# Sending two of every sixteen row tiles from HBM to HBM, one register-addressed row per DMA, in a rank-and-scatter kernel that is bound by its DMA engines

## The chip, the cores and the metric

The kernel runs on one core of one Trainium2 chip. The metric is the device time of one execution, in microseconds, and lower is better. A run of several executions is given by its median. SP, ACT, Pool and VectorE are engines of the core; the sequencers of SP, ACT and Pool, which run their instructions, also issue the DMAs. Sixteen DMA engines move the data in packets. A DMA has landed when the last of its sixteen completion counts, one from each DMA engine, has arrived.

## The reference

```python
def setup_inputs():
    B, N, D = 8, 2048, 2560
    return {"x": np.random.randn(B, N, D).astype(np.float32),
            "scores": np.random.randn(B, N).astype(np.float32)}

def reference(x, scores):
    ranks = np.argsort(np.argsort(scores, axis=1), axis=1)
    out[b_idx, ranks, :] = x        # out has the shape of x
```

Row `i` of a batch goes to row `rank(score i)` of the output. There are 16,384 rows of 2,560 floats (10,240 bytes), so 167.8 MB are read and 167.8 MB written. The arithmetic is small; the kernel is a permutation of rows.

## The kernel before

The scores are spread over all partitions, and VectorE counts for each row of a 128-row tile how many scores precede it. One tile takes three comparisons with an accumulator and three small instructions that join the counts:

```python
    def compute_ranks_for_batch(b):
        for k in range(T):                      # T = 16 tiles of P = 128 rows
            ... tensor_scalar(is_lt, add)  -> accA   # later scores
            ... tensor_scalar(is_le, add)  -> accB   # earlier scores
            ... scalar_tensor_tensor       -> accC   # ties inside the tile
            ... tensor_tensor(add) twice   -> rank_f32[:, col]
            nc.vector.tensor_copy(out=ranks_i32[:, col:col+1], in_=rank_f32[:, col:col+1])
```

The data path is a load into SBUF, issued by SP, and a scatter, issued by Pool, whose row addresses are the ranks:

```python
    for b in range(B):
        for t in range(T):
            xt = x_pool.tile([P, D], fp32, tag="x")          # 13 buffers
            nc.sync.dma_start(out=xt[:], in_=x[b, P*t:P*(t+1), :])
            nc.gpsimd.indirect_dma_start(                    # cut
                out=out_flat, out_offset=IndirectOffsetOnAxis(ap=ranks_i32[:, col:col+1], axis=0),
                in_=xt[:], element_offset=b*N*D, ...)
```

Of the kernel before, what the change touches and what calls it, by code (L numbers as in the profile page):

```python
# [10 lines left out]
@with_exitstack  # L11
def kernel(
    ctx: ExitStack,
    tc: tile.TileContext,
    x: bass.AP,
    scores: bass.AP,
    out: bass.AP,
):
    nc = tc.nc
    fp32 = mybir.dt.float32  # L20
    i32 = mybir.dt.int32

    B, N, D = x.shape
    P = 128
    T = N // P

    out_flat = out.flatten_outer_dims()

    const_pool = ctx.enter_context(tc.tile_pool(name="const", bufs=1))
    rank_pool = ctx.enter_context(tc.tile_pool(name="rank", bufs=1))  # L30
    NXBUF = 13
    x_pool = ctx.enter_context(tc.tile_pool(name="x", bufs=NXBUF))
    psum_pool = ctx.enter_context(tc.tile_pool(name="bc_psum", bufs=8, space=bass.MemoryType.PSUM))

    s_all = const_pool.tile([P, B * N], fp32, name="s_all")
    s_col = const_pool.tile([P, B * T], fp32, name="s_col")
    NR = B * T
    s_rows = const_pool.tile([NR, P], fp32, name="s_rows")
    ones128 = const_pool.tile([P, P], fp32, name="ones128")
    tri128 = const_pool.tile([P, P], fp32, name="tri128")  # L40
    ident128 = const_pool.tile([P, P], fp32, name="ident128")
    trash = const_pool.tile([P, N], fp32, name="trash")

    accA = rank_pool.tile([P, B * T], fp32, name="accA")
    accB = rank_pool.tile([P, B * T], fp32, name="accB")
    accC = rank_pool.tile([P, B * T], fp32, name="accC")
    rank_f32 = rank_pool.tile([P, B * T], fp32, name="rank_f32")
    ranks_i32 = rank_pool.tile([P, B * T], i32, name="ranks_i32")

    nc.sync.dma_start(  # L50
        out=s_rows[:],
        in_=scores.rearrange("b (k p) -> (b k) p", p=P),
    )

    nc.gpsimd.memset(ones128[:], 1.0)  # L55
    nc.gpsimd.affine_select(  # L56
        out=tri128[:],
        in_=ones128[:],
        pattern=[[-1, P]],
        compare_op=mybir.AluOpType.is_ge,  # L60
        fill=0.0,
        base=-1,
        channel_multiplier=1,
    )
    make_identity(nc, ident128[:])

    scol_psum = psum_pool.tile([P, 512], fp32, tag="bc")
    nc.tensor.transpose(  # L68
        out=scol_psum[:, :NR],
        in_=s_rows[:],  # L70
        identity=ident128[:NR, :NR],
    )
    nc.scalar.copy(out=s_col[:], in_=scol_psum[:, :NR])  # L73

    GRP = 4
    n_groups = (T + GRP - 1) // GRP
    for b in range(B):
        for g in range(n_groups):
            k_lo = GRP * g
            k_hi = min(T, k_lo + GRP)  # L80
            nk = k_hi - k_lo
            bc_psum = psum_pool.tile([P, 512], fp32, tag="bc")
            for j in range(nk):
                k = k_lo + j
                col = b * T + k
                nc.tensor.transpose(  # L86
                    out=bc_psum[:, P * j: P * (j + 1)],
                    in_=s_col[:, col:col + 1].to_broadcast([P, P]),
                    identity=ident128[:],
                )  # L90
            nc.scalar.copy(  # L91
                out=s_all[:, b * N + P * k_lo: b * N + P * k_hi],
                in_=bc_psum[:, :P * nk],
            )

    def compute_ranks_for_batch(b):
        base = b * N
        for k in range(T):
            col = b * T + k
            sc = s_col[:, col:col + 1]  # L100
            nc.vector.tensor_scalar(  # L101
                out=trash[:, :N - P * k],
                in0=s_all[:, base + P * k: base + N],
                scalar1=sc,
                scalar2=None,
                op0=mybir.AluOpType.is_lt,
                op1=mybir.AluOpType.add,
                accum_out=accA[:, col:col + 1],
            )
            if k > 0:  # L110
                nc.vector.tensor_scalar(  # L111
                    out=trash[:, :P * k],
                    in0=s_all[:, base: base + P * k],
                    scalar1=sc,
                    scalar2=None,
                    op0=mybir.AluOpType.is_le,
                    op1=mybir.AluOpType.add,
                    accum_out=accB[:, col:col + 1],
                )
            nc.vector.scalar_tensor_tensor(  # L120
                out=trash[:, :P],
                in0=s_all[:, base + P * k: base + P * (k + 1)],
                scalar=sc,
                in1=tri128[:],
                op0=mybir.AluOpType.is_equal,
                op1=mybir.AluOpType.mult,
                accum_out=accC[:, col:col + 1],
            )
            if k > 0:
                nc.vector.tensor_tensor(  # L130
                    out=rank_f32[:, col:col + 1],
                    in0=accA[:, col:col + 1],
                    in1=accB[:, col:col + 1],
                    op=mybir.AluOpType.add,
                )
                nc.vector.tensor_tensor(  # L136
                    out=rank_f32[:, col:col + 1],
                    in0=rank_f32[:, col:col + 1],
                    in1=accC[:, col:col + 1],
                    op=mybir.AluOpType.add,  # L140
                )
            else:
                nc.vector.tensor_tensor(  # L143
                    out=rank_f32[:, col:col + 1],
                    in0=accA[:, col:col + 1],
                    in1=accC[:, col:col + 1],
                    op=mybir.AluOpType.add,
                )
            nc.vector.tensor_copy(  # L149
                out=ranks_i32[:, col:col + 1],  # L150
                in_=rank_f32[:, col:col + 1],
            )

    for b in range(B):
        compute_ranks_for_batch(b)

    span = B * N * D
    for b in range(B):
        for t in range(T):
            col = b * T + t  # L160
            xt = x_pool.tile([P, D], fp32, name=f"xt_{b}_{t}", tag="x")
            nc.sync.dma_start(out=xt[:], in_=x[b, P * t: P * (t + 1), :])  # L162
            scatter_out = dataclasses.replace(
                out_flat[:], dep_tracking_offset=col * span
            )
            nc.gpsimd.indirect_dma_start(  # L166
                out=scatter_out,
                out_offset=bass.IndirectOffsetOnAxis(
                    ap=ranks_i32[:, col:col + 1], axis=0
                ),  # L170
                in_=xt[:],
                in_offset=None,
                element_offset=b * N * D,
            )


# [28 lines left out]
```

## Time and profile before

| | before |
|---|---|
| median | 796.45 us (796.38 to 796.53, 2 runs) |
| bytes through the DMA engines | 335.75 MB, 429 GB/s in all but the first and last slice |
| VectorE / Pool / ACT / PE busy | 49% / 15% / 2% / 2% |

These are lines of the page of the kernel before: the busy tenths and the GB/s in 40 equal slices of the span, the DMA queues (packets, MB, share of the time of 16 engines), the chain of waits that ended last by line, and the DMA issues (count, KB each, median us from issue to landing).

```profile
DVE  6999999999999999999900000000000000000000
DMA  8999999999999999999999999999999999999996
GB/s 345 429 429 428 429 428 429 429 428 429 428 428 428 429 428 429 428 428 429 428 429 429 429 429 429 429 429 429 429 429 429 428 429 429 429 429 430 429 429 260
q1 hardware_dynamic: 18576, 167.85, 50.0%
q0 software_dynamic: 18432, 167.78, 49.8%
DMA xt<-in_x_dram 96%; SPq L162 0%; POOLq L200 0%; SPq L50 0%; POOLq L166 0%
xt<-in_x_dram SPq DMA_DIRECT2D x128, 1280.0 KB, 48.8
out_dram<-xt,ranks_i POOLq DMA_INDIRECT x128, 28.2
```

The DMA engines work without a gap. SP's loads and Pool's scatters take half of them each, because every byte passes twice. A DMA lands 28 to 49 us after its issue and nobody minds: the buffers keep enough of them in flight.

### The profile page before, as it was taken

The page shows a single profiled execution, that of the slowest core. Times are in us where ns is not written, and L with a number is a line of the kernel's source. Part 1 is how long each engine was busy: PE and PEld are TensorE (multiplying, and loading weights), DVE is VectorE, ACT ScalarE, POOL GpSimd, SP SyncE. Part 2 cuts the span into 40 slices and gives each one's busy share as a digit, 9 for nine tenths or more (in the row PEclk, how much of TensorE's full clock was granted, in tenths as well). Part 3 has the DMA queues.
Part 4 walks back from the last instruction along what each step waited for, and adds up shares of the span by engine and source line. Part 5 has one row for each costly group of instructions (what it writes and reads, how often), then busy time and mean ns, then how long its engine had stood idle before and what let it go on. Part 6 is the DMA issues. An engine that isn't in the chain of part 4 may idle for free.

```text
span 794.8 us, 1987 instructions
## 1 busy us (share of the span) xinstructions
PE 15.9 (2%) x129; PEld 15.4 (2%) x129; DVE 388.0 (49%) x1128; ACT 17.5 (2%) x34; POOL 123.0 (15%) x136
## 2 busy tenths in 40 slices
PE   7000000000000000000000000000000000000000
PEld 7000000000000000000000000000000000000000
DVE  6999999999999999999900000000000000000000
ACT  8000000000000000000000000000000000000000
POOL 1211111111111111111111111111111111111110
PEclk9555555555555555555555555555555555555555
DMA  8999999999999999999999999999999999999996
GB/s 345 429 429 428 429 428 429 429 428 429 428 428 428 429 428 429 428 428 429 428 429 429 429 429 429 429 429 429 429 429 429 428 429 429 429 429 430 429 429 260
DMA packets 37023, 335.75 MB, mean 422 GB/s; under 512 B 4113, under 2 KB 4241, under 8 KB 4241
## 3 DMA queue, kind: packets, MB, share of 16 engines
q1 hardware_dynamic: 18576, 167.85, 50.0%
q0 software_dynamic: 18432, 167.78, 49.8%
q14 instruction: 14, 0.11, 0.0%
q8 instruction: 1, 0.02, 0.0%
HBM read 167.84 MB, written 167.77 MB: 422 GB/s over the span
## 4 chain that ended last, share of the span: by engine, by line
DMA 96%; another core or an unknown queue 1%; SPq 1%; issue 0%; POOLq 0%
DMA xt<-in_x_dram 96%; SPq L162 0%; POOLq L200 0%; SPq L50 0%; POOLq L166 0%
## 5 line engine op out<-in xcount | busy, mean ns | idle before, releaser
L166 POOL DMA_INDIRECT out_dram<-xt,ranks_i x128 | 121.9, 952 | 656.7 <-DMA xt<-in_x_dram 425.4
L101 DVE TENSOR_SCALAR_CACHE_REDUCE trash<-s_all,s_col 128x2048 f32<-128x2048 f32 (+15 forms) x128 | 172.1, 1345 | 8.0 <-ACT s_all L91 7.6
L111 DVE TENSOR_SCALAR_CACHE_REDUCE trash<-s_all,s_col 128x128 f32<-128x128 f32 (+14 forms) x120 | 153.5, 1279 | 0.0
L120 DVE SCALAR_TENSOR_TENSOR trash<-s_all,s_col,tri 128x128 f32<-128x128 f32 x128 | 45.0, 351 | 0.4
L149 DVE CAST ranks_i<-rank_f 128x1 int32<-128x1 f32 x128 | 19.0, 149 | 0.0
L130 DVE TENSOR_TENSOR rank_f<-accA,accB 128x1 f32<-128x1 f32 x120 | 18.7, 156 | 0.0
L136 DVE TENSOR_TENSOR rank_f<-rank_f,accC 128x1 f32<-128x1 f32 x120 | 18.6, 155 | 0.0
L91 ACT COPY s_all<-bc_psum 128x512 f32<-128x512 f32 x32 | 16.0, 749 | 1.7 <-PE bc_psum L86 1.7
L86 PE MATMUL bc_psum<-ident,s_col 128*128 128x128 f32 x128 | 15.4, 286 | 0.4 <-ACT s_col L73 0.4
L86 PEld LDWEIGHTS bc_psum<-ident,s_col 128*128 128x128 f32 x128 | 15.2, 146 | 0.6 <-ACT s_col L73 0.6
L120 DVE DVE_READ_ACCUMULATOR trash<-s_all,s_col,tri 128x1 f32 x128 | 10.6, 83 | 0.0
L101 DVE DVE_READ_ACCUMULATOR trash<-s_all,s_col 128x1 f32 x128 | 10.5, 82 | 0.0
L111 DVE DVE_READ_ACCUMULATOR trash<-s_all,s_col 128x1 f32 x120 | 9.9, 83 | 0.0
L73 ACT ACT_TABLE_LOAD x1 | 1.3, 1283 | 0.8 <-PEq L189 0.8
L143 DVE TENSOR_TENSOR rank_f<-accA,accC 128x1 f32<-128x1 f32 x8 | 1.3, 159 | 0.0
L68 PE MATMUL scol_psum<-ident,s_rows 128*128 128x128 f32 x1 | 0.4, 448 | 2.9 <-DMA s_rows<-in_scores_dram 2.9
L73 ACT COPY s_col<-scol_psum 128x128 f32<-128x128 f32 x1 | 0.3, 266 | 1.3 <-PE scol_psum L68 1.3
L56 POOL TENSOR_SCALAR_AFFINE_SELECT tri<-ones 128x128 f32<-128x128 f32 x1 | 0.3, 283 | 0.0
masks.py:199 POOL TENSOR_SCALAR_AFFINE_SELECT ident<-ident 128x128 f32<-128x128 f32 x1 | 0.3, 282 | 0.0
L55 POOL MEMSET ones<- 128x128 f32 x1 | 0.2, 205 | 0.3 <-POOLq L189 0.3
L68 PEld LDWEIGHTS scol_psum<-ident,s_rows 128*128 128x128 f32 x1 | 0.2, 183 | 2.9 <-issue 2.9
masks.py:197 POOL MEMSET ident<- 128x128 f32 x1 | 0.2, 202 | 0.0
(4 smaller groups left out, 0.4 us busy)
## 6 DMA issues: line engine op xcount, KB each, us to landing
xt<-in_x_dram SPq DMA_DIRECT2D x128, 1280.0 KB, 48.8
out_dram<-xt,ranks_i POOLq DMA_INDIRECT x128, 28.2
s_rows<-in_scores_dram SPq DMA_DIRECT2D x1, 64.0 KB, 2.0
```

Of the source, the lines that this page charges most:

```text
L68: nc.tensor.transpose(out=scol_psum[:, :NR], in_=s_rows[:], identity=ident128[:NR, :NR],)
L73: nc.scalar.copy(out=s_col[:], in_=scol_psum[:, :NR])
L86: nc.tensor.transpose(out=bc_psum[:, P * j: P * (j + 1)], in_=s_col[:, col:col + 1].to_broadcast([P, P]), identity=ident128[:],)
L91: nc.scalar.copy(out=s_all[:, b * N + P * k_lo: b * N + P * k_hi], in_=bc_psum[:, :P * nk],)
L101: nc.vector.tensor_scalar(out=trash[:, :N - P * k], in0=s_all[:, base + P * k: base + N], scalar1=sc, scalar2=None, op0=mybir.AluOpType.is_lt,
L111: nc.vector.tensor_scalar(out=trash[:, :P * k], in0=s_all[:, base: base + P * k], scalar1=sc, scalar2=None, op0=mybir.AluOpType.is_le, op1 ...
L120: nc.vector.scalar_tensor_tensor(out=trash[:, :P], in0=s_all[:, base + P * k: base + P * (k + 1)], scalar=sc, in1=tri128[:], op0=mybir.Alu ...
L130: nc.vector.tensor_tensor(out=rank_f32[:, col:col + 1], in0=accA[:, col:col + 1], in1=accB[:, col:col + 1], op=mybir.AluOpType.add,)
L136: nc.vector.tensor_tensor(out=rank_f32[:, col:col + 1], in0=rank_f32[:, col:col + 1], in1=accC[:, col:col + 1], op=mybir.AluOpType.add,)
L143: nc.vector.tensor_tensor(out=rank_f32[:, col:col + 1], in0=accA[:, col:col + 1], in1=accC[:, col:col + 1], op=mybir.AluOpType.add,)
L149: nc.vector.tensor_copy(out=ranks_i32[:, col:col + 1], in_=rank_f32[:, col:col + 1],)
L166: nc.gpsimd.indirect_dma_start(out=scatter_out, out_offset=bass.IndirectOffsetOnAxis(ap=ranks_i32[:, col:col + 1], axis=0), in_=xt[:], in_ ...
```

## The change

The intent is to take bytes off the bottleneck. Two of the sixteen tiles of each batch (2,048 rows in all) no longer go through SBUF: each row is one DMA from `x` in HBM to its place in `out` in HBM, so its bytes pass the engines once. The target row sits in a register, loaded sixteen at a time. SP issues the rows of one tile and ACT those of the other. Pool issues loads and scatters of the other 112 tiles ("the bulk").

```diff
-    NXBUF = 13
+    NXBUF = 12
     ...
+    DIRECT = (T - 2, T - 1)
+    G = 16
     for b in range(B):
-        compute_ranks_for_batch(b)
+        compute_ranks(b, DIRECT)
+        ... transpose the two rank columns to rows_i[2, P], cast to int32
+        compute_ranks(b, BULK)
+
+    def direct_rows(eng, et, b, q, g):
+        _, vals = nc.values_load_multi_w_load_instructions(
+            rows[b][q:q + 1, G * g: G * (g + 1)], engines=[et], ...)
+        for i in range(G):
+            r = P * DIRECT[q] + G * g + i
+            o = dataclasses.replace(out[b, bass.ds(vals[i], 1), :], ...)
+            eng.dma_start(out=o, in_=x[b, r:r + 1, :])
     ... (cut: load(k) and scatter(k) now both on nc.gpsimd)
+    with tc.manual_schedule(engines={ACT, SPE, POOLE}):
+        for k in range(LEAD): load(k)                 # LEAD = 8
+        for k in range(len(bulk)):
+            if k + LEAD < len(bulk): load(k + LEAD)
+            scatter(k)
+        for b in range(B):
+            for g in range(P // G):
+                direct_rows(nc.sync, SPE, b, 0, g)
+                direct_rows(nc.scalar, ACT, b, 1, g)
```

More of the change, by code (lines that the diff above doesn't have):

```diff
@@ L94, with compute_ranks @@
             )
-    def compute_ranks_for_batch(b):
+    def compute_ranks(b, tiles):
         base = b * N
-        for k in range(T):
+        for k in tiles:
             col = b * T + k
@@ L152, in compute_ranks_for_batch @@
             )
-    for b in range(B):
-        compute_ranks_for_batch(b)
-    span = B * N * D
-    for b in range(B):
-        for t in range(T):
-            col = b * T + t
-            xt = x_pool.tile([P, D], fp32, name=f"xt_{b}_{t}", tag="x")
-            nc.sync.dma_start(out=xt[:], in_=x[b, P * t: P * (t + 1), :])
-            scatter_out = dataclasses.replace(
-                out_flat[:], dep_tracking_offset=col * span
-            )
-            nc.gpsimd.indirect_dma_start(
-                out=scatter_out,
-                out_offset=bass.IndirectOffsetOnAxis(
-                    ap=ranks_i32[:, col:col + 1], axis=0
-                ),
-                in_=xt[:],
-                in_offset=None,
-                element_offset=b * N * D,
-            )
+    span = B * N * D
@@ new lines @@
+    ACT = mybir.EngineType.Activation
+    SPE = mybir.EngineType.SP
+    DIRECT = (T - 2, T - 1)
+    BULK = [t for t in range(T) if t not in DIRECT]
+    G = 16
+    drow_pool = ctx.enter_context(tc.tile_pool(name="drow", bufs=2))
+    rows = []
+    for b in range(B):
+        compute_ranks(b, DIRECT)
+        rp = psum_pool.tile([P, 512], fp32, tag="bc", name=f"rp_{b}")
+        rows_i = drow_pool.tile([len(DIRECT), P], i32, tag="rows", name=f"rows_{b}")
+        nc.tensor.transpose(
+            out=rp[:len(DIRECT), :P],
+            in_=rank_f32[:, b * T + DIRECT[0]: b * T + T],
+            identity=ident128[:],
+        )
+        nc.vector.tensor_copy(out=rows_i[:], in_=rp[:len(DIRECT), :P])
+        rows.append(rows_i)
+        compute_ranks(b, BULK)
@@ new lines, in direct_rows @@
+    def direct_rows(eng, et, b, q, g):
+        _, vals = nc.values_load_multi_w_load_instructions(
+            rows[b][q:q + 1, G * g: G * (g + 1)],
+            engines=[et],
+            min_val=0,
+            max_val=N - 1,
+            skip_runtime_bounds_check_because=(
+                "a rank counts other scores of one row of N, so it lies in 0..N-1"
+            ),
+        )
+        t = DIRECT[q]
+        for i in range(G):
+            r = P * t + G * g + i
+            o = dataclasses.replace(
+                out[b, bass.ds(vals[i], 1), :],
+                dep_tracking_offset=(B * T + b * N + r) * span,
+            )
+            eng.dma_start(out=o, in_=x[b, r:r + 1, :])
@@ new lines, with load, scatter @@
+    POOLE = mybir.EngineType.Pool
+    bulk = [(b, t) for b in range(B) for t in BULK]
+    LEAD = 8
+    xts = {}
+    def load(k):
+        b, t = bulk[k]
+        xts[k] = x_pool.tile([P, D], fp32, name=f"xt_{b}_{t}", tag="x")
+        nc.gpsimd.dma_start(out=xts[k][:], in_=x[b, P * t: P * (t + 1), :])
+    def scatter(k):
+        b, t = bulk[k]
+        col = b * T + t
+        nc.gpsimd.indirect_dma_start(
+            out=dataclasses.replace(
+                out_flat[:], dep_tracking_offset=col * span
+            ),
+            out_offset=bass.IndirectOffsetOnAxis(
+                ap=ranks_i32[:, col:col + 1], axis=0
+            ),
+            in_=xts.pop(k)[:],
+            in_offset=None,
+            element_offset=b * N * D,
+        )
@@ L178 @@
+    with tc.manual_schedule(engines={ACT, SPE, POOLE}):
+        for k in range(LEAD):
+            load(k)
+        for k in range(len(bulk)):
+            if k + LEAD < len(bulk):
+                load(k + LEAD)
+            scatter(k)
[3 more added lines that the diff above has]
+                direct_rows(nc.scalar, ACT, b, 1, g)
 _INS = ['x', 'scores']
```

## The prediction

Its sums came to 683 + 74 + 14, about 770 us, with the rows hidden, and otherwise to about 755 us for the bulk and a tail of 25 to 180 us. The numbers it starts from are in the trace of the kernel before: bulk packets start 381 ns apart, pieces of 512 bytes take 27 ns and semaphore packets 9, and of 28,234 packets of loads and scatters between 100 and 700 us, 99% were followed on their engine by a packet of the other queue (strung together by their times, as in part 5).

> **What bounds the kernel now.** The chain of waits is 96% DMA of the row-tile loads; the 40-slice table shows the DMA engines at 9 tenths throughout and 429 GB/s, while DVE is busy 49%, POOL 15%, ACT and PE 2%. Each byte passes the DMA engines twice (load, scatter). The packet records show why: each of the 16 engines moves 10,240-byte packets 381 ns apart, 2 x 128 tiles x 8 = 2,048 per engine = 781 us; about 14 us is start and end.
>
> **What the change does.** 112 of 128 tiles keep the double trip: 1,792 packets x 381 ns = 683 us per engine, now all on Pool's queue (8 DMAs in flight, each about 3.05 us of engine time, so that queue should not run dry; Pool's 224 issues of about 0.95 us cost it about 213 us, hidden). 2,048 rows pass once, each as 16 pieces of 640 bytes plus 16 semaphore packets. The 512-byte pieces of the scores load took 27 ns, semaphore packets 9 ns in slots of about 6; I estimate 30 + 6 ns per row and engine, 74 us. Sum 683 + 74 + 14 = about 770 us (-3.3%), if the direct rows are hidden entirely beside the bulk. DVE does the same comparisons (3.05 us per tile, done near 390 us); the eight extra transposes and casts are negligible. DVE's casts of batches 2 and 3 wait for the direct rows of batches 0 and 1 to be read; at my cadence these are done in time.
>
> **The direct rows' own pace decides.** SP and ACT must issue 1,024 rows each in about 735 us: 0.72 us per row. Limits:
> - Turns. In the packet records, the load queue and the scatter queue alternate strictly, packet by packet, and a semaphore packet takes a turn of its own. A direct row then needs two turns, each behind one Pool packet: with 2,016 Pool packets in all (semaphores included), about 0.75 us per row. Bulk ends with at best about 985 of 1,024 rows done on each queue.
> - Window. The built program lets each queue have four rows in flight (each issue waits for the fourth before it). Unloaded pieces: issue 0.33-0.42 us, 0.63 us to the first packet, 0.3-0.5 us from semaphore packet to landing. That fits, but the first scatter needed 3.8 us from issue end to first packet under load. If rows meet that, the cadence exceeds 1 us.
> - Register loads: one of 16 values per 16 rows.[...]
>
> So bulk should end near 755 us and a tail of 40 to 300 direct rows per queue follow at about 0.6 us (issue bound): 25 to 180 us. If data and semaphore share a turn, no tail: 770. A design this finely balanced suggests somebody tuned it to win, so I pull the middle down: 800 us, range 762 to 900; faster 0.38, same 0.24, slower 0.38.
>
> **What would show it.** Right: DMA slices below 9 tenths at the end, with Pool's queue finished and only SP/ACT rows left; DMA-issue median of a direct row about 3 us; SP waiting on its own DMAs. Share of engine time of the direct queues about 9-10%; total bytes 315 MB. Wrong on the good side: SP and ACT finish before Pool, DMA at 9 tenths to the end.
>
> **What would make it wrong.** [...]register-addressed issue well over 0.5 us (slower); 640-byte HBM-to-HBM pieces costing more than 30 ns (slower); packets joined (faster); DVE blocked on the casts, starving scatters (slower).

## The result

| | before | after |
|---|---|---|
| median | 796.45 us | 1,166.88 us (1,165.41 to 1,168.36, 2 runs) |
| bytes | 335.75 MB | 315.31 MB |
| bulk finished at | 792 us | 758 us |
| direct rows issued by then, of 1,024 | | SP 524, ACT 510 |

The ratio is 1.465 (95% interval 1.461 to 1.470). A ratio here is the mean time of one kernel's runs over that of the other's runs of the same rounds, so it is not quite the ratio of the medians quoted. (The end of the bulk is the start of its last packet in the trace.)

The same lines of the page of the changed kernel, which has one queue more; the chain is here given by engine:

```profile
DVE  7999996999995950000000000000000000000000
DMA  9999999999999999999999999511111111111111
GB/s 373 411 422 421 421 422 421 422 421 423 420 421 423 420 422 422 422 419 398 385 372 390 386 382 397 231 27 26 27 27 26 27 27 26 27 27 26 27 27 20
q0 software_dynamic: 32256, 293.62, 61.0%
q1 hardware_dynamic: 32912, 10.62, 4.3%
q10 hardware_dynamic: 32768, 10.55, 4.2%
DMA 56%; ACTq 18%; DVE 4%; issue 3%; PE 0%; ACT 0%; DVEq 0%
out_dram<-in_x_dram SPq DMA_DIRECT2D x1024, 10.0 KB, 4.9
out_dram<-in_x_dram ACTq DMA_DIRECT2D x1024, 10.0 KB, 2.4
```

The reader should see two kernels in this page. Until slice 26 the engines are full, much as before. Then they move 27 GB/s for 400 us: only direct rows are left. The medians 4.9 and 2.4 mix the two stages, and must be taken apart. The next lines are the direct rows' issues in the window 100 to 500 us, with their median time to landing:

```profile
out_dram<-in_x_dram SPq DMA_DIRECT2D x300, 10.0 KB, 5.1
out_dram<-in_x_dram ACTq DMA_DIRECT2D x292, 10.0 KB, 5.2
```

and the same for 540 to 700 us, where the bulk itself ran slower, with the total of that window:

```profile
DMA packets 13070, 61.44 MB, mean 384 GB/s; under 512 B 3995, under 2 KB 7276, under 8 KB 7276
out_dram<-in_x_dram SPq DMA_DIRECT2D x106, 10.0 KB, 5.9
out_dram<-in_x_dram ACTq DMA_DIRECT2D x100, 10.0 KB, 6.2
```

and for 770 to 1,150 us, with no bulk:

```profile
DMA packets 31117, 10.19 MB, mean 27 GB/s; under 512 B 15546, under 2 KB 31095, under 8 KB 31095
out_dram<-in_x_dram SPq DMA_DIRECT2D x486, 10.0 KB, 1.9
out_dram<-in_x_dram ACTq DMA_DIRECT2D x486, 10.0 KB, 2.0
```

300 rows in 400 us is one row per 1.33 us; 486 in 380 us is one per 0.78 us. Beside the bulk a row lands 5.2 us after its issue, and with four rows in flight on a queue (the built program gives each queue four completion semaphores, and an issue waits for the fourth before it; in the trace SP's 1,024 issues use four semaphores, 256 each) the next can be issued every 5.2 / 4 = 1.3 us. That this is what SP waits for is in its own waits (total us, number, longest):

```profile
SPq L193 <- DMA out_dram<-in_x_dram: 277.0, 313, 2.8
```

After the bulk the latency is 2.0 us and the window would allow 0.5 us. Now the sequencer is the limit: 517 ns for an issue (524 on ACT), about 0.7 us with the register arithmetic and gaps, and one register load of 0.97 us (1.02 on ACT) per sixteen rows, which makes 0.78 us. The sum closes: 758 us, plus 510 rows times 0.78 us, is 1,156 us against a span of 1,163.7 us.

The first theory was therefore **W**, the window: latency beside the bulk over four. Rivals were **Q**, SP and ACT hindering each other in something they share; **T**, turns, each direct row waiting for its turns behind bulk packets; and a path of the memory made slow by the scatters' writes.

### The profile page after: what moved, and what is told of

It is laid out like the page before. It is cut to its first block, busy times and chain, and to the rows that moved or that the text cites. A ratio compares the mean times of both kernels' runs of the same rounds, so it can differ in the third digit from the quotient of the medians.

```text
span 1163.7 us, 8140 instructions
## 1 busy us (share of the span) xinstructions
PE 19.7 (2%) x137; PEld 17.1 (1%) x137; DVE 390.0 (34%) x1136; ACT 17.8 (2%) x34; POOL 172.4 (15%) x232
## 2 busy tenths in 40 slices
DMA packets 97999, 315.31 MB, mean 271 GB/s; under 512 B 36368, under 2 KB 69264, under 8 KB 69264
## 4 chain that ended last, share of the span: by engine, by line
DMA 56%; ACTq 18%; DVE 4%; issue 3%; PE 0%; ACT 0%; DVEq 0%
DMA out_dram<-in_x_dram 55%; ACTq L193 15%; ACTq L177 4%; DVE trash L101 2%; DVE trash L111 2%; DVE trash L120 0%; PE bc_psum L86 0%; DMA s_rows<-in_scores_dram 0%; DVE rank_f L130 0%; DVE rank_f L136 0%; DVE ranks_i L149 0%; DVE rows L172 0%; ACT s_all L91 0%; PE scol_psum L68 0%; ACT s_col L73 0%
## 5 line engine op out<-in xcount | busy, mean ns | idle before, releaser
L101 DVE TENSOR_SCALAR_CACHE_REDUCE trash<-s_all,s_col 128x256 f32<-128x256 f32 (+15 forms) x128 | 172.2, 1345 | 8.3 <-ACT s_all L91 7.9
L111 DVE TENSOR_SCALAR_CACHE_REDUCE trash<-s_all,s_col 128x1792 f32<-128x1792 f32 (+14 forms) x120 | 153.4, 1279 | 0.0
L203 POOL DMA_DIRECT2D xt<-in_x_dram x112 | 60.4, 541 | 491.2 <-DMA out_dram<-xt,ranks_i 488.6
L208 POOL DMA_INDIRECT out_dram<-xt,ranks_i x112 | 110.9, 990 | 69.3 <-issue 27.6
L167 PE MATMUL rp<-ident,rank_f 128*2 128x128 f32 x8 | 2.9, 359 | 361.8 <-DVE rank_f L136 361.8
```

What stands on the lines that cost most here:

```text
L101: nc.vector.tensor_scalar(out=trash[:, :N - P * k], in0=s_all[:, base + P * k: base + N], scalar1=sc, scalar2=None, op0=mybir.AluOpType.is_lt,
L111: nc.vector.tensor_scalar(out=trash[:, :P * k], in0=s_all[:, base: base + P * k], scalar1=sc, scalar2=None, op0=mybir.AluOpType.is_le, op1 ...
L203: nc.gpsimd.dma_start(out=xts[k][:], in_=x[b, P * t: P * (t + 1), :])
L208: nc.gpsimd.indirect_dma_start(out=dataclasses.replace(out_flat[:], dep_tracking_offset=col * span), out_offset=bass.IndirectOffsetOnAxis( ...
```

## The experiments

Eighteen kernels ran. "Wrong" marks kernels that leave out work to isolate a cost. A latency is from the start of the issue to the landing, and a cadence is the mean distance of two rows' issues on one queue, both from the trace. Unless noted, edits are against the changed kernel.

### 1. The rows alone, and the bulk alone

`direct_only` (wrong on purpose, one look):

```diff
     with tc.manual_schedule(...):
-        for k in range(LEAD): load(k)
-        for k in range(len(bulk)): ... load(k + LEAD); scatter(k)
         for b in range(B): ... direct_rows(...)
```

> Wrong result on purpose: the bulk is left out, only the 2,048 direct rows are moved. My theory (W): while Pool's 10,240-byte packets fill the DMA engines a row takes about 5.2 us from issue to landing, and with four rows in flight per queue that makes 1.3 us per row; without them the sequencer's own work decides (0.52 us DMA issue + 0.18 us register work and gaps + 1.0 us register load per 16 rows = 0.78 us per row), on SP and ACT at once. So 0.78 us per row from the first row on, latency 1.9 to 2.1 us, span 38 + 1,024 x 0.78 + a few = about 845 us (825 to 870), that is, longer than the whole kernel before. Rival (Q): SP and ACT [...]hold each other up, or the rows are slow in themselves: cadence stays near 1.3 us and the span near 1,370 us.

Measured: 842.31 us. The latency was 2.0 us and the cadence 0.78 us from the start to the end, as in the changed kernel's tail. The direct rows in the window 100 to 500 us:

```profile
out_dram<-in_x_dram SPq DMA_DIRECT2D x503, 10.0 KB, 2.0
out_dram<-in_x_dram ACTq DMA_DIRECT2D x502, 10.0 KB, 2.0
```

Both queues run at full pace beside each other, so Q falls. And this settles something more basic: 1,024 rows per queue need 1,024 x 0.78 = 800 us even on an idle machine. The design could not win at two tiles per batch, whatever the bulk did.

`bulk_only` (wrong on purpose, one look):

```diff
-                direct_rows(nc.sync, SPE, b, 0, g)
-                direct_rows(nc.scalar, ACT, b, 1, g)
+                pass
```

> Wrong result on purpose: the direct rows are left out, 112 tiles go through Pool alone. 1,792 packets x 381 ns = 683 us + 14 us = about 698 us (690 to 705) at 429 GB/s throughout, if the bulk's slower stretch from 520 to 730 us in the changed kernel comes from the direct rows beside it. If it belongs to the bulk (its queue or its addresses), the dip is here too and the span is 715 to 735 us.

Measured: 698.83 us, at 429 GB/s throughout. The bulk's packet sum in the prediction was right (683 + 14 = 697), and Pool issuing both directions costs nothing. There was no slow stretch either, so that of the changed kernel (384 GB/s from 540 to 700 us) comes with the rows or with their instructions.

### 2. Packet size and turns

`half_packets` (correct, one look) cuts the bulk's rows into packets of 5,120 bytes:

```diff
-        nc.gpsimd.dma_start(out=xts[k][:], in_=x[b, ...])
+        nc.gpsimd.dma_start(out=xts[k][:], in_=x[b, ...], max_dma_last_dim=4 * (D // 2))
     ... and two scatters a tile, of half rows, with ranks 2r and 2r + 1
```

> The changed kernel with every bulk row cut in two pieces of 5,120 bytes, for loads and scatters; the direct rows are as they were. Theory W with packets counted: a newly issued row stands behind a fixed number of Pool packets already taken up by the engine (3.3 us from end of issue to first packet = 8 to 9 packets of 381 ns). Halved packets then halve that: first packet about 1.7 us after issue, latency about 3.2 us, cadence 0.8 to 0.9 us while the bulk runs, total 880 to 960 us. Rival (T), turns alone as I predicted: two turns of about 0.2 us per row, so the issue bound of 0.78 us holds at once and the total is about 845 us. Rival (M), a latency of memory or fabric under load that does not depend on packet size: nothing changes, cadence 1.3 us, total about 1,165 us.

Measured: 1,222.06 us, far above the 880 to 960 expected; latency 5.8 to 5.9 us on SP (6.0 on ACT), cadence 1.55 to 1.67 us. The bulk ended at 763 us, 5 us later than in the changed kernel, and only 448 to 456 rows of a queue were issued by then. If a row waited for a fixed number of bulk packets, halving the packets would have halved the wait. It did not, so a fixed number of packets falls, and with it T in its plain form.

`single_packet` (correct, one look) asks for the row's DMA to be one packet, so that its data and its semaphore might share a turn:

```diff
-            eng.dma_start(out=o, in_=x[b, r:r + 1, :])
+            eng.dma_start(out=o, in_=x[b, r:r + 1, :], single_packet=True)
```

> The changed kernel with the option single_packet set on the direct rows, meant to put the 640-byte piece and its semaphore into one packet, so that a row takes one turn per engine and not two. If turns are a large part of the 5.2 us (I estimate 0.8 to 1.6 us of it), the latency beside the bulk falls to 3.6 to 4.4 us and the cadence to 0.9 to 1.1 us, total 960 to 1,060 us. If the start delay (3.2 us from end of issue to the first packet) is what counts and is not shortened, 4.8 to 5.2 us and 1,120 to 1,165 us.

Measured: 1,168.43 us, latency 5.2 us, cadence 1.34 us, and the same 97,999 packets on its page: no change. The option joined no packets, so this run says nothing about turns; `half_packets` is what speaks against them. The prediction's hope for "packets joined" was empty.

### 3. The window itself

`one_tile` (correct, 5 rounds) makes one tile per batch direct, shared by SP and ACT:

```diff
-    DIRECT = (T - 2, T - 1)
+    DIRECT = (T - 1,)
     ...
-            for g in range(P // G):
+            for g in range(0, P // G, 2):
                 direct_rows(nc.sync, SPE, b, 0, g)
-                direct_rows(nc.scalar, ACT, b, 1, g)
+                direct_rows(nc.scalar, ACT, b, 0, g + 1)
```

> One direct tile per batch in place of two, its rows shared by SP and ACT: 512 rows on each queue. Theory W: 34 + 512 x 1.35 = 725 us, so the rows end before the bulk and are hidden; the engines' sum is 1,920 packets x 381 ns = 732 us + half of 74 us + 14 us = 783 us, 1.7% below the kernel before (777 to 795). If the rows slow the bulk as much as in the changed kernel (bulk ended at 758 us where 722 would follow from the sum), about 800 us. Rival (Q): no difference in cadence, also hidden.

Measured: 812.96 us (809.49 to 814.21, 6 runs), ratio 1.021 (1.020 to 1.022). The rows were hidden, the last at 766 us, and still the kernel is 2% slower than before. That was a miss of 30 us, taken up in part 5.

`one_tile_sp` (correct, one look) lets SP issue all of them; the program then has eight rows in flight on that queue instead of four (eight completion semaphores in the built program, with 128 of the 1,024 issues each):

```diff
-                direct_rows(nc.scalar, ACT, b, 0, g + 1)
+                direct_rows(nc.sync, SPE, b, 0, g + 1)
```

> One direct tile per batch, all of its 1,024 rows from SP, which then has all eight completion semaphores and so eight rows in flight in place of four. Theory W (cadence beside the bulk = latency / rows in flight, 5.2 us / 4 = 1.3 us): the window stops binding and the next limits come, issue 0.78 us plus slower register loads, so 0.8 to 0.95 us per row and latency 6 to 7.5 us; all rows at 34 + 1,024 x 0.88 = about 935 us (890 to 980), with the tail after the bulk's end near 790 us. Rival: SP's own work or the engines' turns set the 1.35 us, and the window does not: cadence stays at 1.3 to 1.4 us beside the bulk, about 570 rows done when the bulk ends, total about 1,150 us.

Measured: 910.93 us. Latency stayed at 5.5 to 6.1 us, but the cadence fell from 1.3 us to between 0.80 and 0.91, which is near SP's own 0.78. The rows issued in the window 100 to 500 us (landing records are incomplete in this trace and some others, so the view prints no time; the latency is taken from the last count before a semaphore's next use):

```profile
out_dram<-in_x_dram SPq DMA_DIRECT2D x483, 10.0 KB
```

Doubling the queue's rows in flight removed the wait with the latency nearly unchanged. The pace of all rows together even fell, from 592 to 483 in these 400 us, without a shorter latency, so the rows were not queueing up for something that the two queues share. This confirms W: the pace was the latency over the window.

### 4. What makes a row late beside the bulk

`loads_only` (wrong on purpose, one look) has no scatters:

```diff
-            scatter(k)
```

> Wrong result on purpose: the bulk's scatters are left out, its 112 loads stay and keep the engines full for about 350 us (112 x 3.05 us + rows). The row latency beside them tells what the start delay of 3.2 us is. If it comes from packets or bytes that an engine has already taken up (read-ahead), it is the same here: latency 5 to 5.5 us, cadence 1.3 us. If it comes from writes to HBM (scatters) under load, it falls to about 3 us here and the cadence to about 0.8 us. After the loads end, 0.78 us per row. Total: 34 + 1,024 rows, of which about 240 at 1.33 and 784 at 0.78 = about 965 us in the first case, about 860 us in the second.

Measured: 978.02 us; beside the loads the latency was 5.0 to 5.1 us and the cadence 1.26 to 1.31 us until 300 us. The bulk's writes to HBM are not needed for the delay.

`scatters_only` was to be the opposite and was refused by the check for a race: its wrong ranks let a scatter and a direct row write the same output row. It is no run. It had on record:

> Wrong result on purpose: eight tiles are loaded once and the 112 scatters write them again and again, with the ranks of batch 0, so that nothing but the queue holds them back; about 350 us of scatters alone. Read-ahead in the engine: the same latency, 5 to 5.5 us, cadence 1.3 us, total about 965 us. Writes to HBM under load: the same or more, since all traffic now is such writes. Writes into SBUF as the cause: the latency falls here to about 3 us, total about 860 us.

`scatters_only2` kept the right ranks (wrong, because it scatters eight old tiles again and again):

```diff
-            in_=xts.pop(k)[:],
+            in_=xts[k % LEAD][:],
     ...
-            if k + LEAD < len(bulk):
-                load(k + LEAD)
```

> The experiment that the check refused, mended: eight tiles are loaded once and scattered again and again, now with each tile's own ranks (wrong data on purpose). VectorE yields a tile's ranks every 3.05 us, as fast as the engines can scatter, so they are nearly full for about 400 us. loads_only left the latency at 5.0 us; read-ahead in the engines predicts 4.5 to 5.3 us here too, writes into SBUF as the cause about 3 us, writes to HBM 5.2 us or more. Total 900 to 990 us.

Measured: 1,022.71 us, above the 900 to 990 expected, because the scatters did not keep the engines full (362 GB/s from 100 to 300 us) and lasted until 443 us; latency 4.4 to 6.0 us beside them on SP, cadence 1.25 to 1.6 us. The bulk's writes to SBUF are not needed either. Either direction of bulk alone delays the rows.

Two things were left: **E**, each DMA engine makes a row's piece wait behind data that it has already taken on for the other queue; or **L**, a memory path that all engines share is slow under load. I tried to load only half of the engines.

`half_engines` and `all_engines` (wrong on purpose, one look each) let ACT issue loads of 8 or 16 partitions beside SP's rows:

```diff
-        ... load(k), scatter(k), direct_rows(nc.scalar, ...)
+        for k in range(512):
+            nc.scalar.dma_start(out=xk[j:j + K], in_=blocks[k % nblk])   # K = 8 or 16 partitions x 40 KB
```

> Wrong on purpose: no scatters; only SP's 1,024 direct rows, beside plain loads that ACT issues from 8-partition pieces, so that they should run on 8 of the 16 DMA engines (about 215 GB/s), while a row still uses all 16. Theory E (the row waits behind what each DMA engine has taken on for its other queue): row latency about 5 us and cadence about 1.3 us, as beside the full bulk, and within one row eight of the sixteen landing increments come about 3 us before the other eight. Theory L (loaded HBM or a loaded path shared by all engines makes every access late): at half the load latency 2 to 3.5 us, cadence 0.8 to 0.9 us, all sixteen increments within about 1 us.

> Wrong on purpose: the control of half_engines, the same but with loads of 16-partition pieces, so on all 16 engines (about 425 GB/s). Both theories: latency about 5 us, cadence about 1.3 us, sixteen increments close together. If the latency is near 2 us here, the delay belongs to Pool's queue and half_engines decides nothing.

Measured: 1,902.13 and 3,731.71 us. Neither ran as meant. The loads went out one at a time, about 20 us apart, because each waited for the DMA of a direct row, so there was no steady load, and the planned comparison of latencies decides nothing. But each load put a single packet of 40,960 bytes on an engine, which held it for 4.7 us, and that is a clean event. In `half_engines`, 100 rows met such a packet on eight engines (landing over 4.5 us, not counting 49 rows whose issue itself was held up for 5.1 us). The median arrival of their sixteen landing increments was 2.15 us for the eighth, 6.6 us for the ninth and 7.4 us for the last. The eight engines without a load were on time. The lateness belongs to the individual engine, in this sparse setting.

`pool_half` and `pool_all` (wrong on purpose, one look each) repeat it with a steady load, issued by Pool as the bulk is:

```diff
-        ... load(k), scatter(k)
+        for k in range(512):
+            nc.gpsimd.dma_start(out=xk[j:j + 8], in_=blocks[k], max_dma_last_dim=4 * D)
+            nc.gpsimd.dma_start(out=turn[:, 4*k:4*k + 4], in_=blocks[k][:, 0, 0:4])   # pool_half only
```

> Wrong on purpose: no scatters; the direct rows of SP and ACT as in the changed kernel, beside Pool loads of 8 partitions x 4 pieces of 10,240 bytes, each followed by a 16-byte-a-partition load[...], so that the large ones should all fall on the same eight engines (steady, up to 215 GB/s). Theory E (a row's piece waits for what its own DMA engine has taken on): row latency about 5 us, cadence about 1.3 us, and in a row the eighth landing increment comes near 2 us and the ninth to sixteenth between 4 and 5.5 us. Theory L (a memory path loaded for all): the sixteen increments stay within about 1 us of each other, latency 2 to 3.5 us. If large loads alternate between the halves, no split and a latency in between: then it decides nothing.

> Wrong on purpose: the control of pool_half without the small loads, so that the large ones [...]load all sixteen (about 425 GB/s). Both theories: latency about 5 us, cadence 1.3 us, the sixteen increments within about 1 us of each other while the loads run (about 390 us), 2.0 us and 0.78 us after them.

Measured: 1,988.03 and 1,958.88 us. Loads into eight partitions at a time ran at about a quarter of the speed, with all sixteen engines busy in both kernels. (Eight partitions alone are not the reason: in `half_engines`, after the rows had ended, ACT's loads of eight partitions moved 210 GB/s on eight engines between 1,330 and 1,550 us, while its loads of sixteen partitions in `all_engines` moved 114 GB/s between 2,000 and 3,600 us. The reason stays open.) So `pool_half` shows no half that is free, and the split that it was built for is inconclusive. But the slow loads test E and L in another way. The window 100 to 500 us of `pool_all` (queue, packets, MB, share of 16 engines; then the issues):

```profile
DMA packets 17848, 48.04 MB, mean 120 GB/s; under 512 B 10037, under 2 KB 13367, under 8 KB 13367
q0 software_dynamic: 11186, 45.82, 96.9%
out_dram<-in_x_dram SPq DMA_DIRECT2D x104, 10.0 KB, 15.3
out_dram<-in_x_dram ACTq DMA_DIRECT2D x104, 10.0 KB, 15.3
```

Only 120 GB/s moved, against 422 beside the bulk, and yet a row took 15.3 us instead of 5.2. Over an unloaded row's 2.0 us, the delay can be counted in the time of one bulk packet on one engine (medians of the packet records):

| kernel | bulk packet | its time | row's extra latency | in packets | in KB |
|---|---|---|---|---|---|
| changed | 10,240 B | 385 ns | 3.2 us | 8 | 85 |
| `half_packets` | 5,120 B | 196 ns | 3.85 us | 20 | 100 |
| `pool_all` | 10,240 B | 1,352 ns | 13.3 us | 10 | 101 |
| `pool_half` | 10,240 B | 1,461 ns | 10.3 us | 7 | 72 |
| `loads_only` | 10,240 B | 385 ns | 3.0 us | 8 | 80 |

A row waits while its engine moves about 70 to 100 KB of the other queue's data, whether the packets are large or small, fast or slow. This agrees with E and not with L, which asked for a shorter delay when less was moved. A shared path that these slow loads themselves clog is not excluded by it; against that stands only `half_engines`, with its sparse loads. So E is the likelier of the two and not shown for the steady bulk. What the engine takes on ahead, and in which part of it, no record shows.

### 5. Why hidden rows gained nothing

`one_tile` was to save 8 x 1.7 us and lost 16 us. Its GB/s line shows both a slow stretch and a thin end:

```profile
GB/s 350 412 423 419 423 420 421 422 421 421 423 422 420 421 423 421 421 422 421 422 422 422 423 421 420 414 385 389 393 389 394 395 389 396 402 394 385 405 428 103
```

`one_tile_rev` (correct, one look, against `one_tile`) takes the batches from last to first, in case the slow stretch belongs to certain addresses:

```diff
-    for b in range(B):            # in all four loops
+    for b in reversed(range(B)):
```

> One direct tile per batch as in one_tile, but the batches are taken from the last to the first, by ranks, bulk and rows alike. It asks about the stretch of one_tile in which the bulk runs slower although the rows came no faster: from 510 us on the bulk moved 385 to 400 GB/s instead of 422, packets of over 420 ns appeared, and one engine ended 13 us after the others. If addresses decide (what lies in batches 5 to 7), the slow stretch comes first here, from the first rows to about 280 us, and 422 GB/s after it. If time or progress decides, it begins near 510 us again. Total near 810 us either way.

Measured: 812.82 us, with the slow stretch from 515 us again. It is not the addresses.

`one_tile_dve` (correct, 3 rounds, against `one_tile`) keeps VectorE busy through that stretch, in case it begins because VectorE falls idle near 400 us:

```diff
+    for _ in range(160):
+        nc.vector.tensor_scalar(out=trash[:], in0=s_all[:, (B-1)*N:B*N], ..., accum_out=idle_acc[:])
```

> one_tile with 160 needless compares at the end of VectorE's program, so that it does not fall idle near 420 us. In the traces so far the slow stretch began after VectorE had finished its ranks (last rank 394 us, slow from 425; 422 and 510 to 515; 421 and 485; 494 and 610). If VectorE's idleness has to do with it, the stretch is gone and the total falls to about 783 us (775 to 790), 1.7% below the kernel before; if it is a coincidence, 810 to 814 us as one_tile.

Measured: 820.04 us (818.43 to 823.26), ratio 1.031 (1.028 to 1.033) against before. The slow stretch stays. It is not VectorE's idleness; the added instructions even cost 7 us.

That cost pointed to the instructions. The records of the landings show that the sixteen engines do not finish a tile's DMA together: one falls steadily behind. In the kernel before, its distance to the first landing grows from 2 to 7 us until VectorE has finished, and then stays; the DMA queue for instructions (q14 of the page) brought eleven packets of 8,192 bytes in that time. In `one_tile`, which has 37 such packets, 28 of them by 520 us, because every direct row adds three instructions (register arithmetic, a move and the DMA; the trace of the changed kernel has 1,024 of each on SP and on ACT), it grows to 17 us by 520 us, where the slow stretch begins. Theory **F**: each packet of instructions puts one engine about 0.5 us back, and the kernel ends with that engine.

`before_fetch` (correct, 3 rounds, against the kernel before) adds instructions that move no data:

```diff
+    for i in range(2048):
+        nc.scalar.copy(out=act_dummy[:, 1:2], in_=s_col[:, 0:1])
```

> The kernel before, plus 2,048 one-column ACT copies that move no data by DMA and feed nothing; correct. Theory F (each packet of instruction fetch delays one DMA engine by about 0.5 us, and that engine is what the span waits for): 2,049 more instructions of 64 bytes are about 131 KB, 16 more fetch packets, so one engine ends about 8 us later: 804 us (801 to 808), ratio about 1.010, with one engine alone working for the last several us. Rival (ACT was idle 98% of the time, so instructions that touch nothing are free): 796.5 us, ratio 1.000.

Measured: 798.02 us (797.94 to 798.34), ratio 1.0019 (1.0003 to 1.0036). The effect is there, but 1.5 us instead of 8. Its page shows 29 packets of instructions instead of 14: 15 packets of 8,192 bytes for 2,049 instructions, about 60 bytes each, where the expectation counted 64. The landings say why: the last engine moved only from 7.3 to 8.1 us behind, but the second to last from 4.6 to 8.0 and the third from 1.3 to 6.8. ACT's instructions seem to burden another DMA engine than VectorE's.

`half_tile` (correct, 3 rounds) makes one tile in every second batch direct:

```diff
-    DIRECT = (T - 2, T - 1)
+    DIRECT = (T - 1,)
+    HAS = [b % 2 == 0 for b in range(B)]
     ... and half of the tile's groups from SP, half from ACT, as in one_tile
```

> One direct tile in every second batch, 4 of 128 tiles, 256 rows from SP and 256 from ACT; correct. Cadence of 1.3 to 1.4 us beside the bulk: rows done by about 400 us, hidden. Theory F (on the engine that serves the instruction fetch a direct tile saves 6.1 us of packets, costs 4.4 us of pieces and semaphores and about 1.6 us of fetch): 4 tiles gain almost nothing, 796 us (793 to 800), ratio 0.995 to 1.004. Rival (the plain packet sum, 1.7 us a tile gained): 790 us, ratio 0.991.

Measured: 796.71 us (796.54 to 797.1), ratio 1.0001 (0.9985 to 1.0018). The plain sum of packets, 790, is missed. Of its 6.7 us of gain, about 5 went into the end: the landings of a scatter end 12.2 us apart, against 7.3 before. The last 15 us of it:

```profile
GB/s 300 328 219 218 191 164 137 137 137 109 55 55 55 55 55 55 55 55 55 55 55 55 27 27 27 27 27 27 27 27 27 27 0 0 0 0 0 0 0 0
```

Sixteen engines move 429 GB/s, so 27 GB/s is one engine. Here two and then one work on for 8 us while the others have nothing to do.

`before_fetch_dve` (correct, 3 rounds, against the kernel before) puts the 2,048 instructions on VectorE, after its last rank:

```diff
+    for i in range(2048):
+        nc.vector.tensor_copy(out=idle[:, 1:2], in_=rank_f32[:, B*T-1:B*T])
```

> The kernel before, plus 2,048 one-column VectorE copies after the last rank; correct. before_fetch gave +1.5 us and left two DMA engines 8 us behind instead of one. Theory F2 (each issuing engine's instructions are fetched through a DMA engine of its own, and each 8,192-byte packet puts that one back by 0.5 us): VectorE's 11 packets and 16 more fall on one engine, which ends about 8 us later than before: 804 us (801 to 807), ratio about 1.010. Rival (fetching costs about 0.1 us a packet wherever it falls): 798 us, ratio 1.002.

Measured: 809.07 us (808.88 to 809.39), ratio 1.0158 (1.0141 to 1.0175): 12.6 us, above the range that F2 gave, and far from the rival's 798. The distance of the last engine went to 17 us at 700 us and to 21 at the last loads. Pool's issues took 0.95 us each as before, so the copies did not hold up Pool. So the direction holds and the size was underestimated: 12.6 us / 2,048 is 6.1 ns an instruction, 0.8 us a packet of 8,192 bytes.

The records do not name the engine of a packet, but beside a full load a packet starts just as the one before it on its engine ends (in the kernel before, records of 385 ns start 381 ns apart), so they can be strung together by their times. In `before_fetch_dve` the string with eleven packets of instructions had begun 1,147 bulk packets at 450 us, and the other fifteen strings 1,165 to 1,168: the engine that brings VectorE's instructions is the one that lags, by about 18 bulk packets of 381 ns, or 0.6 us for each packet of instructions. In `before_fetch`, 13 of ACT's packets lie on one string (994 bulk packets at 390 us, against 1,004 to 1,011), and VectorE's on others.

`before_lean` (correct, 5 rounds, against the kernel before) is the same in reverse, and a candidate to beat both kernels. The instructions that join the counts are done for up to eight tiles at once:

```diff
+    nc.gpsimd.memset(accB[:], 0.0)
+    ends = [groups([1, 1, 1, 1, 4, 8] if b == 0 else [8, 8]) for b in range(B)]
     ...
-            nc.vector.tensor_tensor(out=rank_f32[:, col:col + 1], ...)   # and so on, per tile
+            if k ends a group g of columns:
+                nc.vector.tensor_tensor(out=rank_f32[:, g], in0=accA[:, g], in1=accB[:, g], op=add)
+                nc.vector.tensor_tensor(out=rank_f32[:, g], in0=rank_f32[:, g], in1=accC[:, g], op=add)
+                nc.vector.tensor_copy(out=ranks_i32[:, g], in_=rank_f32[:, g])
```

> The kernel before with the small VectorE instructions that join the counts into a rank (two additions and a cast a tile) done for 4 or 8 tiles at once: 438 VectorE instructions in the program instead of 754; correct. before_fetch_dve cost 12.6 us for 2,048 more VectorE instructions, 6.1 ns each; before has one DMA engine about 7 us behind at the end. Theory F2: 316 fewer instructions give back about 2 us, 794.5 us (793.5 to 795.5), ratio about 0.9975, and the spread of a load's sixteen landings ends near 5 us instead of 7. Rival (VectorE's instructions are free while it is idle half the time): 796.5 us, ratio 1.000.

Measured: 794.54 us (793.93 to 794.69, 5 runs), ratio 0.9974 (0.9959 to 0.9988), as expected. VectorE's busy time fell by 3% (388.0 to 376.7 us), while the last engine's distance fell from 7.3 to 4.2 us: the lag goes with the number of instructions, not with VectorE's work. The end of the kernel before, in its last 15 us, and then of `before_lean`:

```profile
GB/s 410 437 410 437 437 410 437 437 410 437 437 437 410 437 437 410 437 246 109 82 55 55 55 55 27 55 55 27 27 27 27 27 27 27 0 0 0 0 0 0
```

```profile
GB/s 437 437 437 437 410 437 437 437 437 382 437 437 437 437 437 437 410 437 410 410 437 437 437 164 137 82 82 55 55 27 27 27 27 27 0 0 0 0 0 0
```

The thin end is 17 slices of 0.375 us in the first and 11 in the second. `before_lean` is the fastest correct kernel, by a quarter of a per cent.

## Why the prediction was wrong

It said 800 us with a range of 762 to 900; the kernel took 1,166.88 us.

**The step that failed is "Window".** It set the unloaded times, 0.33 to 0.42 us for the issue, 0.63 us to the first packet and 0.3 to 0.5 us to the landing, against four rows in flight and said "That fits". The mechanism was right: `one_tile_sp` shows that the pace is latency over window (1.3 us a row with four in flight; with eight, 0.80 to 0.91, near SP's own 0.78). The mis-sized term is the row's latency beside the bulk. The cadence of 0.75 us that the text went on with needs 3 us ("DMA-issue median of a direct row about 3 us"); it measured 5.2 us, so 1.3 us a row, and 510 to 524 rows of each queue were issued when the bulk ended instead of "at best about 985". The warning was in the prediction: the first scatter had taken 3.8 us from issue to first packet under load. In the changed kernel the first direct row took 3.2 us from the end of its issue to its first packet, and 0.77 us in `direct_only`. I had the loaded number and built the sum on the unloaded one.

**The second mis-sized term is the tail's cadence.** "About 0.6 us (issue bound)" measured 0.78: a register-addressed issue is 0.52 us rather than 0.33 to 0.42, the register arithmetic and gaps bring it to 0.7, and sixteen registers take 0.97 us. This term alone puts two direct tiles above 800 us (`direct_only`), which the prediction could have estimated and did not. The register load was named, but the trace of the kernel before holds no time for one; that of the changed kernel shows 0.97 us unloaded and a median of 1.6 us beside the bulk (SP, 100 to 700 us). Together: a tail of 40 to 300 rows at 0.6 us became one of 510 at 0.78 us.

**Turns were not the limit.** The prediction let a direct row wait for one Pool packet per turn. The packet records of the changed kernel do show the queues taking turns: of 18,929 packets of direct rows between 100 and 500 us, strung together by their times, 97% were followed on their engine by a packet of another queue. But the order of the records is not the wait: `half_packets` and `pool_all` show that a row's wait is no fixed number of turns: it comes to 70 to 100 KB of the other queue's data, some eight of the bulk's packets in the changed kernel and twenty of the half ones, which one packet per turn doesn't tell.

**What was right, and what was luck.** The bulk ended at 758 us (755 predicted), but that is luck: the prediction's sum had nearly all rows beside the bulk, and with the 1,034 that were issued by then it gives 683 + 37 = 720 us. The slow stretch, which nobody predicted, made up the difference. The bytes were 315 MB, the direct queues took 4.3 and 4.2% of the engines' time (8.5% together, "9-10%" predicted), and a row cost an engine about 34 ns (36 estimated): 28 ns from the start of its piece to the next packet and 6 for its semaphore packet. The tail has the shape that was to show the prediction right. VectorE's casts did wait for the rows (550 us in all), but Pool's scatters waited for VectorE only about 23 us.

**The reason given for the middle value was no reason.** The text's own sum, 755 us and a tail of 25 to 180 us, gives 780 to 935. "Somebody tuned it to win" then pulled the middle down to 800, and nothing in the profile said so.

**What stays open.** In `one_tile`, the lag of one engine explains the thin end and its growth goes with the packets of instructions. Why such a packet costs 0.6 us or more is open, since its own record is 0.31 us long. That the bulk slows by some 7% once the lag is at 17 us is not explained by it in full: `before_fetch_dve` lagged by 16 to 20 us from 640 us on and kept 428 GB/s until 760. Nor is the 7 us that 160 VectorE instructions cost in `one_tile_dve`. That ACT's instructions are fetched through another DMA engine than VectorE's is inferred from landings and from packets strung together by time. And E for the steady bulk is argued, as said in part 4.

## What to carry to other kernels

Before moving work from few large DMAs to many small ones with a limited number in flight, take their latency under the load they will run in, and divide it by the number in flight (here 5.2 us over four, 1.3 us a row): that pace, and the sequencer's own pace per issue including register loads (here 0.78 us), must both fit beside the bulk. A DMA that saves bytes is no gain if it arrives in its own tail at 27 GB/s. And in a kernel bound by DMA, count instructions too: here 2,048 VectorE instructions that did nothing cost 12.6 us (on ACT 1.5), and taking away 316 gave back 2.
